# Transposing attention probabilities in one DMA per pair or in two, with another spread of the gate steps

## The chip, the cores and the metric

The kernel runs on one core of a Trainium2 chip. The core has five engines that run their own instruction streams: TensorE (PE; PEld is its weight load), VectorE (DVE), ScalarE (ACT), GpSimd (POOL) and SyncE (SP), which here only issues DMAs. The metric is the device time of one execution in microseconds; smaller is better.

## The reference

One decoder layer over 1024 positions of width 1024. Two groups of eight heads read the same input projection: multi-head latent attention (MLA, causal), and a dilated sliding-window attention in which three windows are mixed. Each group has a SiLU gate; then come one output projection, the residual and a layer norm.

```python
h = x @ w_in
c_q, c_kv, k_rope, g_a, q_b, k_b, v_b, g_b = split(h)
y_a = mla_attention(c_q, c_kv, k_rope, ...) * silu(g_a)      # p = softmax(q k), then p @ v
y_b = dilated_attention(q_b, k_b, v_b) * silu(g_b)           # three dilations, combined
x   = layernorm(ALPHA * x + concat(y_a, y_b) @ w_out)
```

## The kernel before

Products are made in split precision: a high and a low part of each operand, three matmuls (`PASSES`) for each product. The order of work has four stages: the input projections, the dilated attention, MLA, and the output projection with the layer norm.

**Dilated stage.** `steps` lists 32 units `(hp, s, u)`: head pair, half of the sequence, block of 128 queries. For a unit, `dil_scores` (L606, L610) makes the scores of both heads `e`, L614 adds the mask and takes the row minimum on DVE, L620 is the exponential on ACT, `dil_high` (L638 to L643) scales and writes the high fp16 part, `dil_low` (L653, L655) the low part, on POOL or DVE. Both parts of two units that follow each other lie in one tile `p16` (names `p` in the profile). After every second unit one DMA transpose on SP's queue (L658) turns it into `ptd`: 24 blocks of 128x128 where `s` is 0, 32 where `s` is 1. `dil_values` (L686) multiplies the four units of a half with the values into `Od`.

**Gates among the units.** The 16 gates are products of the input with gate weights (L522, 24 matmuls each). They are generators: `next(fill)` does one step, half a gate of 12 matmuls. A unit does one step, and eight of the units do two. When gate (3, 0) is done, the latents `c`, tables and `u` are loaded (L705, L708, L759). After the gates come `gen_kpe`, `gen_k` and `gen_q`, which make the first keys and queries of MLA (L716, L730, L765, L768). Gate weights `wg` come by DMAs on ACT's queue (L116), are split by ACT (L75) and POOL (L76); there are three weight buffers and two for the raw data.

**MLA stage.** 64 units `(hp, ch, e, qi)`: head pair, chunk of 256 queries, head, query block in the chunk. `scores` (L804, L810), `expo` (L815), `high` (L831, L833) and `low` (L840 on POOL, L842 on DVE) give the high and low part of `n = 2*ch + qi + 1` key blocks. The two query blocks `qi` of a row `(hp, ch, e)` lie in one tile `ph` (the tag `p16`, three buffers for both stages), and when both are there, one DMA transpose on SP's queue (L844) turns 2 * (2n - 1) blocks, n that of `qi` 1, into `pT`: 6, 14, 22 or 30 for `ch` 0 to 3. `values` (L854) multiplies `pT` of both heads with the values into `O`.

**Output.** `project` (L953) and L1082 make the output projection from the gated results `ys` and the weights `wo`.

**What sets the order.** The lines above are recorded in program order, and a scheduler with its own costs then places all instructions on their engines; an edit in one place can so move rows anywhere behind it. Each engine then runs its rows strictly in order. DMAs of SP and ACT take eight completion semaphores (DMAHW0 to DMAHW7) in turn; a DMA waits until the one that had its semaphore before it has landed.

Of the kernel before, what the change touches and what calls it, by code (L numbers as in the profile page):

```python
# [40 lines left out]
def tile_hybrid_layer(ctx, tc, xT, xres, w_c, w_c2, w_vr, w_k, w_q, w_g, w_u, w_o,  # L41
                      qg, kvg, ln_g, ln_b, tabs, msk_mla, msk_dil, cs_dil, cs_pe, out):
    nc = tc.nc
    sync = nc.sync
# [281 lines left out]
    def pow2_find(vmx, nm, bank_=bank):  # L326
        m1 = small.tile([P, 1], F32, name=nm + "m1", tag="vm")
        nc.vector.tensor_reduce(m1, vmx, AX.X, ALU.max)
        find_pow2(m1, 2.0 ** -40, nm, bank_)

    def pow2(j, nm, inv, bank_=bank):

        e = common_pow2(nm, bank_)
        r = small.tile([P, 1], F32, name=nm + "r", tag="vm4")
        nc.vector.reciprocal(r, e)
        nc.vector.tensor_scalar(scl[:, j, 0:1], r, 2.0 ** 14, None, ALU.mult)
        nc.vector.tensor_scalar(scl[:, j, 1:2], e, 2.0 ** -14 * inv, None, ALU.mult)
# [63 lines left out]
    def mla_scales():  # L401

        ee, d = fs[:, 4:5], fs[:, 5:6]
        nc.vector.tensor_mul(ee, es[:, 1:2], es[:, 3:4])
        nc.vector.tensor_scalar(scl[:, 0, 1:2], ee, 2.0 ** -5 / PSC, None, ALU.mult)
        nc.vector.tensor_scalar(fs[:, 6:7], scl[:, 4, 1:2], 2.0, None, ALU.mult)
        nc.vector.scalar_tensor_tensor(d, ee, 2.0 ** 10, fs[:, 6:7], ALU.mult, ALU.max)
        nc.vector.reciprocal(fs[:, 6:7], d)
        nc.vector.tensor_scalar(fs[:, 2:3], fs[:, 6:7], 2.0 ** 15, None, ALU.mult)
        nc.vector.tensor_scalar(fs[:, 3:4], fs[:, 2:3], ee, 2.0 ** -24, ALU.mult, ALU.mult)  # L410
        nc.vector.tensor_mul(fs[:, 6:7], es[:, 0:1], es[:, 2:3])
        nc.vector.tensor_scalar(fs[:, 7:8], fs[:, 6:7], d, -SC_MLA * 2.0 ** -19, ALU.mult, ALU.mult)

    def load_qk(hp):
        QQ[hp] = qqp.tile([P, 2, T], F16, name=f"qq{hp}", tag="qq")
        KK[hp] = b8.tile([P, 3, T], F16, name=f"kk{hp}", tag="kk")
        for s in range(2):
            sync.dma_start_transpose(QQ[hp][:, :, half(s)], q_d[half(s), hp * 2 * P:(hp + 1) * 2 * P])
            yield
            sync.dma_start_transpose(KK[hp][:, :, half(s)], k_d[half(s), hp * 3 * P:(hp + 1) * 3 * P])  # L420
            yield
# [130 lines left out]
    VA, VB, TD, ST, P16, PTD = ({} for _ in range(6))  # L552

    def load_v(hp):
        VA[hp] = four(f"vA{hp}", [P, NB, 2, P])
        sync.dma_start(VA[hp], v_d[1][:, :, hp].rearrange("n p l c -> p n l c"))
        VB[hp] = four(f"vB{hp}", [P, 2, 4, 2, P])
        for c in range(4):
            sync.dma_start(VB[hp][32 * c:32 * c + 32].rearrange("a j r l c -> a (j r) (l c)"),
                           v_d[1][2 * c:2 * c + 2].rearrange("j (r a) g l c -> a g (j r) (l c)", a=32)[:, hp])  # L560
# [30 lines left out]
    def dil_scores(u_):  # L591

        hp, s, u = u_
        i, ns = 4 * s + u, 3 + s
        stt = ST[u_] = small.tile([P, 2, 4], F32, name=f"st{hp}{i}", tag="st", bufs=4)
        TD[u_] = four(f"td{hp}{i}", [P, 2, 512], F32)
        S = [ps_s.tile([P, 512], F32, name=f"Sd{hp}{i}{e}", tag="S")[:, :ns * P] for e in range(2)]

        for cls in range(2):
            for w, e in JOBS:  # L600
                rows = ME[e] if w else slice(0, P)
                q, kk = QQ[hp][rows, e], KK[hp][rows, 2 if w else e]
                if not cls:
                    rhs = kk[:, (i - 1) * P:(i + 1) * P] if i else \
                        kk[:, 0:P].unsqueeze(1).broadcast_to([rows.stop - rows.start, 2, P])
                    nc.tensor.matmul(S[e][:, (ns - 2) * P:], q[:, i * P:i * P + P], rhs, start=(w == 0), stop=False)  # L606
                    continue
                for r in range(4):
                    rhs = kk.rearrange("p (i r a) -> p r i a", r=4, a=32)[:, r, 0:4 * s + 4]
                    nc.tensor.matmul(S[e][32 * r:32 * r + 32, :(ns - 2) * P],  # L610
                                     q[:, i * P + 32 * r:i * P + 32 * r + 32], rhs, start=False, stop=(w == 1))
        mk = mdil[:, u if i else 4, (4 - ns) * P:]
        for e in range(2):
            nc.vector.tensor_tensor_reduce(TD[u_][:, e, :ns * P], S[e], mk, dsc[:, 1:2], BIG,  # L614
                                           ALU.add, ALU.min, stt[:, e, 0:1])
# [7 lines left out]
    def dil_inv(u_):  # L623
        stt = ST[u_]
        nc.vector.tensor_scalar(stt[:, :, 2], stt[:, :, 1], 1.0 / PSC, None, ALU.mult)
        nc.vector.reciprocal(stt[:, :, 3], stt[:, :, 2])  # L626

    def dil_high(u_):
        hp, s, u = u_
        ns = 3 + s  # L630
        if u % 2 == 0:
            P16[hp, s] = hp_.tile([P, 2, 2, 2, ns * P], F16, name=f"p16{hp}{s}{u}", tag="p16")
        p16 = P16[hp, s][:, u % 2]
        for e in range(2):
            t, h, sc = TD[u_][:, e, :ns * P], p16[:, e, 0], ST[u_][:, e, 3:4]
            w = WHO[u][e]
            if w == "P":
                nc.gpsimd.tensor_scalar(t, t, sc, 1.0, ALU.mult, ALU.mult)  # L638
                sc = 1.0
            if w == "Q":  # L640
                nc.gpsimd.tensor_scalar(h, t, sc, 1.0, ALU.mult, ALU.mult)
            else:
                nc.scalar.activation(h, t, AF.Copy, scale=sc)  # L643

    def dil_low(u_):
        hp, s, u = u_
        ns, p16 = 3 + s, P16[hp, s][:, u % 2]
        if u == 0:
            PTD[hp, s] = tp.tile([P, 4, 4 * ns, P], F16, name=f"ptd{hp}{s}", tag=f"pT{s}")
        for e in range(2):  # L650
            t = TD[u_][:, e, :ns * P]
            if WHO[u][e] == "P":
                nc.gpsimd.tensor_sub(p16[:, e, 1], t, p16[:, e, 0])  # L653
            else:
                nc.vector.scalar_tensor_tensor(p16[:, e, 1], t, ST[u_][:, e, 3:4], p16[:, e, 0],  # L655
                                               ALU.mult, ALU.subtract)
        if u % 2:
            sync.dma_start_transpose(PTD[hp, s][:, u - 1:u + 1].rearrange("p u z c -> p (u z) c"),  # L658
                                     P16[hp, s].rearrange("p u e l w -> p (u e l w)"))

    def dil_values(hp, s):
        g = GT[4 + hp, s]
# [29 lines left out]
    Q, K, U, PT, SM, TT, V, P16, PB = ({} for _ in range(9))  # L692
# [142 lines left out]
    def low(u):  # L835
        hp, ch, e, qi = u
        n, p16 = 2 * ch + qi + 1, P16[u]
        t = TT[u][:, :n * P].rearrange("p (n c) -> p n c", n=n)
        if n in POOLN:
            nc.gpsimd.tensor_sub(p16[:, :, 1], t, p16[:, :, 0])  # L840
        else:
            nc.vector.scalar_tensor_tensor(p16[:, :, 1], t, SM[u][:, 3:4], p16[:, :, 0], ALU.mult, ALU.subtract)  # L842
        if qi:
            sync.dma_start_transpose(PT[hp, ch][:, e], PB[hp, ch, e].rearrange("p n l c -> p (n l c)"))  # L844

    def values(hp, ch):
        O = gbank(f"O{hp}{ch}")[:, :256]
# [23 lines left out]
    for n in range(ND + 5):  # L871
        cur = steps[n] if n < ND else None
        old = steps[n - 1] if 1 <= n <= ND else None
        if n == 2:
            pow2_find(krm, "kr", gbank)
        if n == 5:
            pow2(4, "kr", 2.0 ** 14, gbank)
            mla_scales()
            nc.vector.tensor_scalar(scl[:, 0, 2:3], scl[:, 0, 1:2], 0.5, None, ALU.mult)
        if cur:  # L880
            if cur[1:] == (0, 1) and 0 < cur[0] < PAIRS - 1:
                qks = load_qk(cur[0] + 1)
            next(qks, None)
            if cur[1:] == (1, 0) and cur[0]:
                load_v(cur[0])
            dil_scores(cur)
        if old:
            dil_inv(old)
            dil_high(old)
            dil_low(old)  # L890
        if cur:
            for e in range(2):
                dil_expo(cur, e)
            for _ in range(1 + (n % 3 == 0 and n < 24)):
                next(fill, None)
        if n == ND + 3:
            for _ in fill:
                pass
        m = n - DV
        if 0 <= m < ND and m % 4 == 3:  # L900
            dil_values(*steps[m][:2])
# [60 lines left out]
    for n in range(NU + 8):  # L962
        if n < NU:
            hp, ch, e, qi = units[n]
            z = n % 16
# [103 lines left out]
    for i in ROWS:  # L1069
# [5 lines left out]
        for c in range(2):  # L1075
            if i in HALVED:
                n = 1 + (i == ROWS[-1])
                for z in ((0, 512),) if n == 1 or c == 0 else ((0, 256), (256, 512)):
                    p = gbank(f"op{i}{c}{z[0]}")
# [119 lines left out]
```

## Time and profile before

| | us |
|---|---|
| median of 3 runs | 653.58 (650.23 to 655.44) |
| profiled execution | 648.14 |
| its span, first to last instruction | 646.3 |
| PE busy | 594.8 (92% of the span) |
| DVE busy | 398.2 (62%) |
| ACT busy | 320.0 (50%) |
| POOL busy | 299.1 (46%) |

Busy is time in which an engine has an instruction under way. A busy PE is not a PE at its peak, since matmuls are pipelined and their ends are modelled. Chain rows tell what the end of the program followed from, step by step; a wait row tells which engine's idle time a given producer ended.

### The profile page before, as it was taken

What the parts mean: (1) busy time and instruction counts of PE and PEld (TensorE: products, weight loads), DVE (VectorE), ACT (ScalarE), POOL (GpSimd) and SP (SyncE); (2) the same over time, 40 slices, a digit from 0 to 9 for tenths busy, and PEclk for the clock granted to TensorE, in tenths of its full rate; (3) what the DMA queues carried; (4) which work ended last, traced back from release to release, by engine and by line L of the source; (5) the groups of instructions that cost most, each with busy time, mean ns of one, the idle gap of its engine ahead of it and who ended that gap; (6) DMA issues with size and microseconds to landing.
All of it is one profiled execution on the core that took longest, in us unless ns stands there. A gap on an engine that the chain in (4) does not pass through costs nothing. (4 is left out here: it accounts for less than half of the span.)

```text
span 646.3 us, 11099 instructions
## 1 busy us (share of the span) xinstructions
PE 594.8 (92%) x4046; PEld 435.7 (67%) x4046; DVE 398.2 (62%) x890; ACT 320.0 (50%) x645; POOL 299.1 (46%) x326
## 2 busy tenths in 40 slices
PE   8999998999999899999997987887989977999995
PEld 5888886788999366776764644434545546778884
DVE  3425318480541686644644897678898997365696
ACT  4452136554221386545636575577978787340000
POOL 3374754265331227534644757373758566450000
PEclk9999999999999999999997997988999987999999
DMA  6666137796012779993999996549798899752042
GB/s 198 188 198 198 30 97 204 221 289 174 33 66 74 260 233 144 184 208 78 225 296 234 184 212 147 108 94 185 150 159 163 173 199 225 185 154 81 17 163 98
DMA packets 198663, 105.52 MB, mean 163 GB/s; under 512 B 157520, under 2 KB 175568, under 8 KB 198480
## 3 DMA queue, kind: packets, MB, share of 16 engines
q1 hardware_dynamic: 195008, 99.11, 64.7%
q10 hardware_dynamic: 3600, 5.71, 3.4%
q8 instruction: 31, 0.51, 0.3%
q14 instruction: 24, 0.20, 0.1%
HBM read 47.65 MB, written 18.35 MB: 102 GB/s over the span
## 5 line engine op out<-in xcount | busy, mean ns | idle before, releaser
L522 PE MATMUL gP<-x,wg 128*128 128x512 f32 x384 | 98.8, 406 | 5.9 <-ACT wg L75 5.5
L522 PEld LDWEIGHTS gP<-x,wg 128*128 128x128 f32 x384 | 70.7, 191 | 23.2 <-ACT wg L75 6.1
L953 PE MATMUL op<-wo,ys 128*128 128x512 f32 x288 | 70.7, 401 | 0.6 <-ACT ys L75 0.4
L953 PEld LDWEIGHTS op<-wo,ys 128*128 128x128 f32 x288 | 54.3, 191 | 14.4 <-ACT ys L75 0.9
L815 ACT ACTIVATE p<-p,sm 128x128 f32<-128x128 f32 (+3 forms) x64 | 49.1, 767 | 22.1 <-DVE sm L810 17.3
L804 PE MATMUL S<-k,q 128*128 128x512 f16 (+3 forms) x288 | 54.7, 339 | 5.2 <-DVE sm L810 4.8
L253 PE MATMUL cP<-x,wc 128*128 128x512 f32 x240 | 56.7, 395 | 0.0
L810 DVE CUSTOM_DVE_ANT_0 p<-S,mask,fs 128x128 f32<-128x128 f32 (+3 forms) x64 | 50.5, 809 | 4.7 <-POOL ph L840 3.4
L253 PEld LDWEIGHTS cP<-x,wc 128*128 128x128 f32 x240 | 44.7, 188 | 10.3
L620 ACT ACTIVATE td<-td,st 128x384 f32<-128x384 f32 (+1 forms) x64 | 42.1, 659 | 16.6 <-DVE st L614 16.4
L638 POOL TENSOR_SCALAR td<-td,st 128x384 f32<-128x384 f32 (+1 forms) x32 | 22.5, 710 | 56.9 <-DVE st L626 44.4
L804 PEld LDWEIGHTS <-q 128*128 128x128 f16 x288 | 26.7, 101 | 30.8 <-issue 5.7
L614 DVE CUSTOM_DVE_ANT_0 td<-Sd,mdil,dsc 128x384 f32<-128x384 f32 (+1 forms) x64 | 41.3, 679 | 9.1 <-PE Sd L610 8.9
L168 PE MATMUL acc<-wq,x 128*128 128x512 f32 x192 | 45.1, 395 | 0.9 <-DVE x L155 0.8
L854 PE MATMUL O<-pT,v 128*64 128x256 f16 (+1 forms) x480 | 33.1, 285 | 13.9 <-DMA pT<-ph 11.4
L129 PE MATMUL qkP<-wk,x 128*128 128x512 f32 x192 | 44.5, 393 | 0.0
L840 POOL TENSOR_TENSOR ph<-p,ph 128x256 f16<-128x256 f32 (+3 forms) x32 | 36.6, 1153 | 15.6 <-ACT ph L833 12.4
L854 PEld LDWEIGHTS <-v 128*64 128x64 f16 x480 | 28.8, 119 | 22.1 <-issue 18.4
L842 DVE SCALAR_TENSOR_TENSOR ph<-p,sm,ph 128x128 f16<-128x128 f32 (+3 forms) x32 | 35.0, 1101 | 13.8 <-ACT ph L833 13.8
L168 PEld LDWEIGHTS acc<-wq,x 128*128 128x128 f32 x192 | 36.0, 188 | 10.5 <-DVE x L155 1.3
L129 PEld LDWEIGHTS qkP<-wk,x 128*128 128x128 f32 x192 | 36.0, 188 | 8.2
L653 POOL TENSOR_TENSOR p<-td,p 128x384 f16<-128x384 f32 (+1 forms) x32 | 35.7, 1124 | 11.4 <-ACT p L643 11.2
(313 smaller groups left out, 1158.7 us busy)
## 6 DMA issues: line engine op xcount, KB each, us to landing
u<-in_w_u_dram SPq DMA_DIRECT2D x20, 256.0 KB, 3.1
v_d<-v SPq DMA_DIRECT2D x16, 256.0 KB, 2.1
wor<-in_w_o_dram SPq DMA_DIRECT2D x8, 512.0 KB, 4.2
xr<-in_xres_dram SPq DMA_DIRECT2D x16, 256.0 KB, 3.1
out_dram<-xr SPq DMA_DIRECT2D x16, 256.0 KB, 2.1
xr<-in_xT_dram SPq DMA_DIRECT2D x15, 256.0 KB, 3.0
k_d<-k SPq DMA_DIRECT2D x8, 384.0 KB, 4.4
c_d<-c SPq DMA_DIRECT2D x10, 256.0 KB, 2.4
```

The costliest lines, as they stand in the source:

```text
L129: nc.tensor.matmul(d, xs[k][i // 4][:, a, (i % 4) * P:(i % 4) * P + P], w8[k][:, b, o:o + w], **flags(k, KD, (a, b)))
L168: nc.tensor.matmul(acc[i], xs[k][i // 4][:, a, (i % 4) * P:(i % 4) * P + P], ws[:, b, :512], start=(k == 0 and (a, b) == (0, 0)), stop=(k ...
L253: nc.tensor.matmul(dst, ww(k, a, m), xs[k][s][:, b], **flags(k, KD, (a, b)))
L522: nc.tensor.matmul(p, wg[k // 4][:, a, (k % 4) * P:(k % 4) * P + P], xs[k][s][:, b], **flags(k, KD, (a, b)))
L614: nc.vector.tensor_tensor_reduce(TD[u_][:, e, :ns * P], S[e], mk, dsc[:, 1:2], BIG, ALU.add, ALU.min, stt[:, e, 0:1])
L620: nc.scalar.activation(t[:, :w], t[:, :w], AF.Exp, bias=ST[u_][:, e, 0:1], scale=-1.0, accum_out=ST[u_][:, e, 1:2])
L804: nc.tensor.matmul(S[:, lo:hi], q[:, a, qc], k[:, b, lo:hi], start=((a, b) == (0, 0)), stop=((a, b) == (1, 0)))
L810: nc.vector.tensor_tensor_reduce(t[:, :w], S[:, :w], M["mask"][:, T - w:], fs[:, 7:8], BIG, ALU.add, ALU.min, sm[:, 0:1])
L815: nc.scalar.activation(TT[u][:, :w], TT[u][:, :w], AF.Exp, bias=SM[u][:, 0:1], scale=-1.0, accum_out=SM[u][:, 1:2])
L840: nc.gpsimd.tensor_sub(p16[:, :, 1], t, p16[:, :, 0])
L854: nc.tensor.matmul(O[ME[e], q0:], V[hp][:, kb, vh, ME[e]], rhs, **flags(kb, 2 * ch + 2, (vh, phl)))
L953: nc.tensor.matmul(op[i][:, half(c)], ys[k][a][:, i * P:(i + 1) * P], ws[k][b][:, half(c)], **flags(n_, KD, (a, b)))
```

## The change

Each transpose becomes two. In the dilated stage each unit is turned by itself (12 or 16 blocks), right after its `dil_low`; in MLA each query block of a row (2n blocks: 2 and 4, 6 and 8, 10 and 12, 14 and 16). Tiles and buffers stay as they are. The number of transposes of probabilities goes from 16 + 32 to 32 + 64, the blocks stay the same. The eight units with two gate steps were units 0, 3, 6, ... 21 and are now 0, 2, 4, ... 14. By either rule the 32 gate steps end with unit 23.

```diff
@@ dil_low
-        if u % 2:
-            sync.dma_start_transpose(PTD[hp, s][:, u - 1:u + 1].rearrange("p u z c -> p (u z) c"),
-                                     P16[hp, s].rearrange("p u e l w -> p (u e l w)"))
+        sync.dma_start_transpose(PTD[hp, s][:, u], p16.rearrange("p e l w -> p (e l w)"))
@@ low
-        if qi:
-            sync.dma_start_transpose(PT[hp, ch][:, e], PB[hp, ch, e].rearrange("p n l c -> p (n l c)"))
+        z = 2 * qi * (n - 1)
+        sync.dma_start_transpose(PT[hp, ch][:, e, z:z + 2 * n], p16.rearrange("p n l c -> p (n l c)"))
@@ main loop of the dilated stage
-            for _ in range(1 + (n % 3 == 0 and n < 24)):
+            for _ in range(1 + (n % 2 == 0 and n < 16)):
                 next(fill, None)
```

Lines behind L658 have a number smaller by 1 or 2 in the changed kernel (L844 is L842, L658 is L657, L708 is L706).

The first place is SP's queue in MLA, at chunks 1 to 3 of the first head pair. A row is one DMA; `pT` is the target, `ph` the tile with the probabilities of one row, and the middle number the blocks. Before:

```order
L844 DMA_TRANSPOSE pT_4755<-ph_4858 128x14x128
L844 DMA_TRANSPOSE pT_4820<-ph_4904 128x22x128
L844 DMA_TRANSPOSE pT_4820<-ph_4964 128x22x128
L844 DMA_TRANSPOSE pT_4922<-ph_4994 128x30x128
L759 DMA u_5610<-u_d_75 128x2048
L844 DMA_TRANSPOSE pT_4922<-ph_5059 128x30x128
```

After the change:

```order
L842 DMA_TRANSPOSE pT_4839<-ph_4924 128x10x128
L842 DMA_TRANSPOSE pT_4772<-ph_4877 128x6x128
L842 DMA_TRANSPOSE pT_4772<-ph_4877 128x8x128
L842 DMA_TRANSPOSE pT_4839<-ph_4924 128x12x128
L842 DMA_TRANSPOSE pT_4839<-ph_4985 128x10x128
L757 DMA u_5202<-u_d_74 128x2048
L842 DMA_TRANSPOSE pT_4839<-ph_4985 128x12x128
L842 DMA_TRANSPOSE pT_4943<-ph_5016 128x14x128
L842 DMA_TRANSPOSE pT_4943<-ph_5016 128x16x128
L842 DMA_TRANSPOSE pT_4943<-ph_5082 128x14x128
L842 DMA_TRANSPOSE pT_4943<-ph_5082 128x16x128
```

Each row has become two, and the 10 blocks of chunk 2 now go ahead of the second head of chunk 1.

The second place is the loading of the latents on SP's queue and of the last gate weights on ACT's, late in the dilated stage, with the semaphores that a row waits for. Before, SP:

```order
L708 DMA c_3660<-c_d_67 128x2048 [waits DMAHW3_49,PE_49]
L708 DMA c_3661<-c_d_68 128x2048 [waits DMAHW4_49,PE_49]
L708 DMA c_3662<-c_d_69 128x2048 [waits DMAHW5_49,PE_49]
L708 DMA c_3663<-c_d_70 128x2048 [waits DMAHW6_49,PE_49]
L708 DMA c_3664<-c_d_71 128x2048 [waits DMAHW7_49,PE_49]
L705 DMA tab<-in_tabs_dram 128x512 [waits DMAHW0_49,PE_49]
L759 DMA u_3667<-u_d_72 128x2048 [waits DMAHW1_49,PE_49]
L705 DMA tab<-in_tabs_dram 128x512 [waits DMAHW2_49]
L556 DMA vA_3694<-v_d_66 128x8x256 [waits DMAHW3_49]
```

Before, ACT, whose next gate weights are `wg20r` and `wg21r`:

```order
L116 DMA wg20r<-in_w_g_dram 128x512 [waits DMAHW5_49,Activation_49]
L643 ACTIVATE p_3651<-td_3624,st_3623 128x384 [waits DVE_49,Activation_49]
L620 ACTIVATE td_3702,st_3701<-td_3702,st_3701 128x512 [waits DVE_49,Pool_49]
L620 ACTIVATE td_3702,st_3701<-td_3702,st_3701 128x512 [waits DVE_49]
L116 DMA wg21r<-in_w_g_dram 128x512 [waits DMAHW3_49]
L532 ACTIVATE g_3753<-gP_3675 128x512 [waits PE_49]
```

After the change, SP:

```order
L706 DMA c_3631<-c_d_67 128x2048 [waits DMAHW0_49,PE_49]
L706 DMA c_3632<-c_d_68 128x2048 [waits DMAHW1_49,PE_49]
L706 DMA c_3633<-c_d_69 128x2048 [waits DMAHW2_49,PE_49]
L657 DMA_TRANSPOSE ptd_3573<-p_3569 128x12x128 [waits DMAHW3_49,DVE_49,DMAHW5_49,PE_49,Pool_49]
L757 DMA u_3638<-u_d_72 128x2048 [waits DMAHW4_49,PE_49]
L706 DMA c_3634<-c_d_70 128x2048 [waits DMAHW5_49]
L706 DMA c_3635<-c_d_71 128x2048 [waits DMAHW6_49]
L657 DMA_TRANSPOSE ptd_3573<-p_3569 128x12x128 [waits DMAHW7_49,DVE_49,Pool_49]
L703 DMA tab<-in_tabs_dram 128x512 [waits DMAHW2_49]
```

After the change, ACT:

```order
L116 DMA wg20r<-in_w_g_dram 128x512 [waits DMAHW0_49]
L643 ACTIVATE p_3693<-td_3596 128x384 [waits DMAHW6_49,Pool_49]
L643 ACTIVATE p_3693<-td_3596 128x384 [waits Pool_49]
L620 ACTIVATE td_3666,st_3665<-td_3666,st_3665 128x384 [waits DVE_49] x2
L116 DMA wg21r<-in_w_g_dram 128x512 [waits DMAHW1_49]
L532 ACTIVATE g_3720<-gP_3646 128x512 [waits PE_49]
```

The semaphore of `wg21r` was last taken by the load of `vA`, behind eight other loads; now by the second of the `c` loads.

The third place is DVE between the last dilated units and the first of MLA: L614 is a score row of the dilated stage, `k` and `qf` are the first keys and queries of MLA. Before (the last score row stands two rows ahead of these):

```order
L625 TENSOR_SCALAR st_4425<-st_4425 128x2
L735 SCALAR_TENSOR_TENSOR k_4062<-kg_4178,fs,k_4062 64x512
L625 TENSOR_SCALAR st_4462<-st_4462 128x2
L914 MEMSET mask 128x1024
L735 SCALAR_TENSOR_TENSOR k_4062<-kg_4225,fs,k_4062 64x512
L626 RECIPROCAL st_4425<-st_4425 128x2
L626 RECIPROCAL st_4462<-st_4462 128x2
L687 SCALAR_TENSOR_TENSOR g_2941<-Od_4542,scl,g_2941 128x512
L625 TENSOR_SCALAR st_4498<-st_4498 128x2
L915 COPY mask<-mmla 128x128
L655 SCALAR_TENSOR_TENSOR p_4453<-td_4296,st_4295,p_4453 128x512
L768 SCALAR_TENSOR_TENSOR qf_4283<-qg_4273,tab 128x512
```

After the change:

```order
L733 SCALAR_TENSOR_TENSOR k_4073<-kg_4238,fs,k_4073 64x512
L614 ISA td_4440,st_4439<-Sd_4441,mdil,dsc 128x512
L614 ISA st_4439 128x1
L625 TENSOR_SCALAR st_4309<-st_4309 128x2
L766 SCALAR_TENSOR_TENSOR qf_4297<-qg_4287,tab 128x512
L614 ISA td_4440,st_4439<-Sd_4442,mdil,dsc 128x512
L614 ISA st_4439 128x1
L614 ISA td_4478,st_4477<-Sd_4479,mdil,dsc 128x512
```

The first `qf` stood behind the last score row of the dilated stage and now stands ahead of the last three units' rows.

## Rows read from the trace of the kernel before

**Rows 1.** Windows by stage: length; busy us of PE, PEld, DVE, ACT, POOL; PEclk; DMA.

```profile
232.00:345.00 113.00, 110.14 (x986) 76.60 (x984) 63.51 (x178) 64.14 (x147) 57.45 (x60) 1.00 0.94 197
345.00:403.00 58.00, 48.36 (x460) 29.37 (x461) 47.29 (x101) 37.79 (x85) 37.54 (x42) 0.88 0.94 184
403.00:458.00 55.00, 44.40 (x357) 24.95 (x357) 39.77 (x99) 39.38 (x86) 28.00 (x32) 0.94 0.70 134
458.00:541.00 83.00, 70.35 (x554) 42.10 (x550) 76.49 (x156) 66.87 (x126) 55.10 (x47) 0.96 0.91 169
541.00:646.30 105.30, 97.02 (x493) 77.73 (x491) 66.81 (x132) 20.10 (x39) 20.55 (x14) 0.97 0.42 129
```

**Rows 2.** Waits of PE over the span: us in total, times, longest.

```profile
PE O L854 <- DMA pT<-ph: 11.4, 6, 2.7
PE gP L522 <- ACT wg L75: 5.5, 2, 4.5
...
PE Od L686 <- DMA ptd<-p: 2.3, 1, 2.3
```

**Rows 3.** Waits for transposes between 403 and 458 us.

```profile
PE O L854 <- DMA pT<-ph: 3.3, 2, 1.9
...
ACT ph L833 <- DMA pT<-ph: 1.9, 1, 1.9
```

**Rows 4.** Waits for transposes between 458 and 541 us.

```profile
PE O L854 <- DMA pT<-ph: 8.1, 4, 2.7
...
ACT ph L833 <- DMA pT<-ph: 2.4, 3, 1.0
```

**Rows 5.** Chain that ended last: start, length, what (DMAs from issue to landing).

```profile
437.52 6.81 DMA pT<-ph
...
476.98 8.24 DMA pT<-ph
...
528.64 11.77 DMA pT<-ph x2
```

**Rows 6.** L844 on SP in four windows: 6 blocks; two of 22; 30; 30.

```profile
L844 SPq DMA_TRANSPOSE pT<-ph x1: 1209/1209/1209, 486.9 to 486.9; - x1
...
DMA to landing us min/median/max: 2.8/2.8/2.8
...
L844 SPq DMA_TRANSPOSE pT<-ph x2: 3370/3377/3384, 468.4 to 471.9; - x2
...
DMA to landing us min/median/max: 5.2/5.3/5.3
...
L844 SPq DMA_TRANSPOSE pT<-ph x1: 5147/5147/5147, 537.4 to 537.4; - x1
...
DMA to landing us min/median/max: 6.5/6.5/6.5
...
L844 SPq DMA_TRANSPOSE pT<-ph x1: 4509/4509/4509, 477.0 to 477.0; - x1
...
DMA to landing us min/median/max: 8.2/8.2/8.2
```

**Rows 7.** Timeline late in the dilated stage: start, length, instruction [idle before <-releaser].

```profile
337.09 0.62 ACT L643 ACTIVATE p<-td,st 128x384 f16<-128x384 f32 x1 [3.49 <-DMA c<-c_d]
...
345.38 0.33 ACTq L116 DMA_DIRECT2D wg21r<-in_w_g_dram  x1
345.76 0.60 ACT L532 ACTIVATE g<-gP 128x512 f32<-128x512 f32 x1 [5.12 <-DMA vA<-v_d]
...
348.04 0.80 PE L522 MATMUL gP<-x,wg 128*128 128x512 f32 x1 [4.54 <-ACT wg L75]
```

**Rows 8.** The window around that wait, columns as in rows 1.

```profile
346.60:353.40 6.80, 5.36 (x19) 3.37 (x20) 5.65 (x18) 5.68 (x15) 3.76 (x4) 0.50 1.16 179
```

**Rows 9.** Timeline of PE: one gate step early in the dilated stage.

```profile
279.71 3.04 PE L522 MATMUL gP<-x,wg 128*128 128x512 f32 x12
```

**Rows 10.** Waits of SP's queue over the span.

```profile
SPq L844 <- POOL ph L840: 25.8, 10, 9.4
```

## The prediction

> **What bounds the kernel now.** I read the stages first [rows 1]. From 232 to 345 us PE is busy in 110.1 of 113.0 us: it is the bound, and what makes data ready sooner there gives nothing. From 345 on PE is idle for 9.6 us (58.00 - 48.36), then 10.6, 12.7 and, in the output stage, 8.3. The work of PE is not changed by this edit, so the time can fall only by these idle times and by stretches at the lower clock (PEclk is 0.88 to 0.96 between 345 and 541). The second column to see is DVE: from 458 to 541 it is busy in 76.5 of 83.0 us. If PE gets its data sooner there, DVE soon holds it again, since its work stays; only 6.5 us can be had. From 403 to 458 DVE is free for 15.2 us and is no such lid.
>
> Then I asked for what PE waits. Transposed probabilities are its largest wait: 11.4 us in six waits in MLA, and 2.3 us in one in the dilated stage [rows 2]. 3.3 us of the six lie ahead of 458, 8.1 behind it, and ACT waits for the same transposes (it needs their source buffer back) 1.9 and 2.4 us [rows 3, 4]. The chain of waits agrees: single transposes stand in it with 6.81, 8.24 and, two together, 11.77 us [rows 5]. The second largest wait of PE is for gate weights, 5.5 us in two [rows 2], of which one is 4.54 us at 348 [rows 7].
>
> **The change part by part.**
>
> *A transpose by size.* With nothing behind them, 6 blocks land 2.8 us after their issue, 22 blocks 5.2, 30 blocks 6.5; they hold SP's queue for 1.21, 3.38 and 5.15 us [rows 6]. (5.2 - 2.8) / 16 and (6.5 - 2.8) / 24 both give some 0.15 us a block, on 1.9 us that each one has. By this the last piece of a row lands sooner than the whole would: 16 blocks for 30 gain 14 x 0.15 = 2.1 us, 12 for 22 gain 1.5, 8 for 14 gain 0.9; in the dilated stage 12 for 24 gain 1.8. The first piece can go while the second query block is still being worked on.
>
> *What the 48 new transposes cost.* The floor on SP's queue is 1.21 us, seen with 6 blocks; pieces of 2 and 4 will not be cheaper. In MLA the 24 rows of chunks 1 to 3 only divide time that the queue spends anyway. The eight rows of chunk 0 take 2 x 1.21 for 1.21: 9.7 us of SP's time, spread over 140 us. What hides it: SP's queue stands waiting for the low parts, 25.8 us for POOL's alone [rows 10]. If that cover were gone, the 9.7 us would delay whatever is queued behind, which are the loads of `u`, `v` and `wo`. I take 0 and keep up to +3 for the range. The Trainium skill speaks against splitting: in "DMA: Bandwidth & Descriptors", Rules for kernel authors, it says to coalesce many small transfers, because under 64 KB one pays mostly overhead, and a piece of two blocks is just 64 KB. By that rule the 48 pieces would cost their 1.9 us each, 91 us of DMA time. The trace bears out the 1.9 us but not that they add up: 22 blocks issued at 471.9 us, 3.5 us behind other 22 that took 5.2 to 5.3 to land, landed as fast as those [rows 6].
>
> *Term 1, MLA ahead of 458 us.* Two waits of PE, 1.9 and 1.4 us in the 3.3 [rows 3], behind 22 and 30 blocks: 1.5 and 1.4 of them can go. ACT's 1.9 us, behind 14 blocks, loses 0.9. That is 3.8 at most; ACT's and PE's waits lie on one chain through the same rows, and what comes next is DVE, which must finish its rows for the following chunk. I take -2.5, with 0 and -3.8 as ends.
>
> *Term 2, MLA from 458 to 541 us.* Of the 8.1 us [rows 4], the longest wait (2.7) is behind 22 blocks and loses 1.5; the other three, 5.4 together, are behind 30, and lose up to 2.1 each, some 5: 6.5 in all. The lid is DVE's 6.5 us of idle time [rows 1], not all of which can be used, as it has its own waits for ACT. I take -3.0, ends 0 and -6.5.
>
> *Term 3, the dilated stage.* The one wait of 2.3 us [rows 2] is behind 24 blocks; 1.8 could go. I take -1.5, ends 0 and -1.8. The other transposes of this stage have no one waiting.
>
> *Term 4, the gate weights at 348 us.* This goes by the rearrangement, not by the split. ACT's queue stood for 3.49 us until a load of `c` had landed, then issued `wg20r`, then stood again for 5.12 us until `vA` had landed, because the DMA of `wg21r` takes over its semaphore. So `wg20r` lay in its buffer while ACT could not split it, and PE waited 4.54 us [rows 7]. Behind that PE ran for 6.8 us at PEclk 0.50, which is 1.2 GHz, with 5.36 us busy [rows 8]: some 2.7 us lost. In the new order both loads take over semaphores of the first two `c` loads, which are ahead of all the others, so the second stop should go. PE also comes to that gate a little sooner after gate (3, 0), which works the other way. Bounds: -7.2 (4.5 + 2.7) if it all goes, 0 if the weights are as late as before. I take -3.5.
>
> *Term 5, the gates' double steps.* A step holds PE for 3.04 us [rows 9]. By the new rule 24 steps instead of 22 fall in the first sixteen units, so two steps, 6.1 us of PE's work, move from units 16 to 23, where PE has room to be idle, into a stretch where PE is full. Nothing is lost while PE is full, but the weights must come faster: the waits for weights ahead of 345 are 5.5 - 4.5 = 1.0 us now, and I expect that to double, +1. And 6.1 us fewer are there to fill PE's idle time behind 345. The first keys and queries of MLA move up into the same stretch, and should fill most of it; I take +1, with -2 and +6 as ends.
>
> Sum: -2.5 - 3.0 - 1.5 - 3.5 + 2.0 = -8.5 us. The profiled execution took 648.14 us, so it would be 639.6. It stands 5.4 us below the median of the runs, 653.58; the same step from there gives **645.1 us**, 1.3% less.
>
> **The rivals.**
>
> *The wait moves to DVE, and the rearrangement gives nothing.* Then PE's waits for transposes turn into waits for score banks, which DVE empties. For it speaks the 92% of DVE from 458 to 541 [rows 1], against it the 15.2 us that DVE is free before. The gain is term 1 alone: 653.6 - 2.5 = 651.
>
> *The gates' new places cost more than they give.* PE would stand for weights ahead of 345, or behind it with nothing to fill: the +6 of term 5 against terms 1 to 3 (-7.0) and no term 4: 652 to 653. For it speaks that PE has caught up with its weights twice already [rows 2]; against it, that 1.0 us in 113 is little.
>
> *Slower: transposes that follow each other hold each other up.* The place is SP's queue in MLA. The 30 blocks issued at 477.0 landed after 8.2 us, not 6.5, with other 30 blocks behind them at once [rows 6]: 1.7 us more. When every row is two pieces, nearly each has one right behind it. If this 1.7 us comes with each piece, it eats the 0.9 to 2.1 us by which the last piece is shorter, and the first piece of the next row is late too, so ACT gets its buffers later than now. Ten waits (six of PE, four of ACT [rows 3, 4]) longer by 0.6 to 1.2 us give +6 to +12: 660 to 666, with 660 as the value. It decides from the point at which a piece of 16 takes over 6.5 us to land. Against it speak the two rows of 22, which did not hold each other up. The Trainium skill has a rule to this end ("Perfetto Trace Analysis", DMA Optimizations): splitting may let a task end sooner if DMA engines are generally idle. Here their share is 0.91 from 458 to 541 [rows 1], so by that rule the gain is in doubt.
>
> **How the numbers follow.** A measurement of this kernel can hardly tell 1% from no change, 6.5 us (647.0 to 660.1 counts as the same). The forecast has 0.53, with 637 to 649 as its own range; 0.46 of it lies below 647. The rival with DVE has 0.22 (0.02 below 647, the rest the same), the one with the gates 0.12 (0.02 of it slower), the slow one 0.13 (0.12 slower, 0.01 the same). Faster 0.48, the same 0.38, slower 0.14. If every term came to its good end, -3.8 - 6.5 - 1.8 - 7.2 - 2 = -21 or 632; I cut the range at 635. Above, it reaches to 658, past the two rivals that stay within 1% and the +3 of the queue; the slow rival is left out for the most part.
>
> **What would show it right or wrong.** PE's waits for `pT` should fall from 11.4 us to 3 to 6, that for `ptd` to under 1, and pieces of 16 blocks should land in 4.2 to 5 us. Around the second load of `wg20r` and `wg21r`, ACT should stand once, not twice, and PE's wait there be under 2 us, with no 6.8 us at half clock behind it. DVE's busy share in MLA should rise. PE should stay over 95% busy up to 345 us; a fall there is the gates' rival. The output stage should be as long as now. Wrong it would be through a new wait that the scheduler's order makes in a place that I have not weighed: every engine's order differs from the dilated stage on.

## The result, and the profile after

The change made the kernel slower: 670.1 us (median of 4 runs, 667.0 to 673.0) against 653.1 (650.2 to 655.4), ratio 1.027, 95% interval 1.022 to 1.031. That is 17 us, where 8.5 less were forecast. The profiled executions lie further apart (672.32 and 648.14), so sums over their stages show some 24 us.

To see where the time goes, both spans are cut where PE had done the same work (its busy time weighted with the granted clock: 240, 300, 340, 380 and 500 us of it). Windows of the kernel before; the columns are as in [rows 1]: length, busy us of PE and of the others, PEclk, DMA share.

```profile
248.00:309.00 61.00, 59.65 (x512) 42.24 (x512) 33.08 (x94) 33.92 (x75) 32.05 (x33) 1.00 0.82 153
309.00:356.00 47.00, 42.46 (x408) 28.30 (x406) 24.07 (x62) 25.39 (x60) 22.49 (x25) 0.93 1.13 247
356.00:406.00 50.00, 42.74 (x428) 25.94 (x421) 41.37 (x85) 30.64 (x70) 33.24 (x38) 0.93 0.92 184
406.00:557.00 151.00, 128.01 (x990) 78.11 (x988) 122.21 (x264) 111.40 (x219) 88.08 (x81) 0.94 0.83 164
557.00:646.30 89.30, 81.41 (x398) 65.46 (x396) 59.40 (x119) 13.20 (x25) 13.49 (x7) 0.98 0.33 107
```

The same work in the changed kernel:

```profile
249.00:320.00 71.00, 64.01 (x491) 45.08 (x490) 31.53 (x85) 33.92 (x75) 33.77 (x34) 0.93 0.78 139
320.00:361.00 41.00, 40.45 (x392) 27.07 (x391) 21.37 (x58) 23.37 (x53) 21.15 (x22) 1.00 0.98 227
361.00:413.00 52.00, 45.10 (x453) 25.47 (x452) 38.04 (x86) 32.77 (x75) 29.28 (x34) 0.87 0.90 185
413.00:578.00 165.00, 133.80 (x1001) 76.43 (x996) 133.74 (x281) 115.14 (x228) 94.39 (x91) 0.90 0.82 159
578.00:670.50 92.50, 84.74 (x414) 68.75 (x412) 58.48 (x120) 13.84 (x26) 14.07 (x8) 0.97 0.36 111
```

Two numbers of each row matter: PE's idle time (length less busy) and what the lower clock costs at most ((1 - PEclk) x length).

| PE's work from/to | before: idle + clock | after: idle + clock |
|---|---|---|
| 240 to 300, first dilated units | 1.3 + 0 | 7.0 + 5.0 |
| 300 to 340 | 4.5 + 3.3 | 0.5 + 0 |
| 340 to 380, last dilated units | 7.3 + 3.5 | 6.9 + 6.8 |
| 380 to 500, MLA | 23.0 + 9.1 | 31.2 + 16.5 |
| 500 to the end | 7.9 + 1.8 | 7.8 + 2.8 |

The second row is the gain that term 4 forecast, and larger. It is lost again in the first row (10.7 us more), where PE was full before, and in MLA (15.6 us more). By the sums of the two columns 9.4 us more are idle (53.4 against 44.0), and up to 13.4 us more (31.1 against 17.7) go to TensorE's lower clock.

PE's waits in the changed kernel (us in total, times, longest; they answer to [rows 2]):

```profile
PE S L802 <- DVE sm L808: 11.6, 12, 4.1
PE Od L684 <- DMA ptd<-p: 10.6, 4, 5.4
PE O L852 <- DMA pT<-ph: 10.0, 4, 5.2
...
PE gP L522 <- ACT wg L75: 3.1, 3, 2.1
```

The waits that the split was to shorten did not shrink: `pT` 10.0 for 11.4, `ptd` 10.6 for 2.3. The first line was, in the kernel before:

```profile
PE S L804 <- DVE sm L810: 4.8, 4, 3.1
```

The first place of the loss is visible in PE's timeline after the change (start, length, instruction, and in brackets the idle time before it):

```profile
259.11 0.64 PE L610 MATMUL Sd<-kk,qq 128*32 128x256 f16 x16
263.56 0.61 PE L684 MATMUL Od<-ptd,vB 128*64 128x128 f16 x7 [3.81 <-DMA ptd<-p]
...
267.53 12.26 PE L522 MATMUL gP<-x,wg 128*128 128x512 f32 x48
```

Seven value matmuls `Od` stand right behind the scores of unit 6, and the scores of unit 7, then 48 gate matmuls and the scores of unit 8 queue behind them. What followed, with columns as above, is half clock (1.2 GHz) with PE nearly always busy:

```profile
263.10:269.90 6.80, 6.34 (x41) 3.65 (x42) 3.06 (x16) 2.50 (x6) 1.40 (x3) 0.50 0.55 112
```

In the kernel before, PE reaches the same `Od` among the scores of unit 8, one and a half units later in its order, and its bulk only behind the 48 gate matmuls; it waits for nothing:

```profile
258.15 0.24 PE L686 MATMUL Od<-ptd,vB 128*64 128x128 f16 x1
...
259.08 0.24 PE L686 MATMUL Od<-ptd,vB 128*64 128x128 f16 x1
259.26 11.17 PE L522 MATMUL gP<-x,wg 128*128 128x512 f32 x48
270.36 0.81 PE L686 MATMUL Od<-ptd,vB 128*64 128x128 f16 x22
```

PE took none of the ready work behind `Od`. The Trainium skill states this ("PSUM — Partial Sum Buffer", Engine vs sequencer instructions): a weight load may overlap matmuls that are in flight, but matmuls start and complete in program order. The trace agrees, with its 3.81 us.

The data is late there too. ACT's order has the split of a gate weight (L75) ahead of the high parts of units 2 and 3, and its load takes 7.6 us (issued 243.0):

```profile
250.68 0.62 ACT L75 CAST wg<-wg51r 128x512 fp32r<-128x512 f32 x1 [5.18 <-DMA wg51r<-in_w_g_dram]
```

Before, the same instruction waited for nothing:

```profile
244.86 0.60 ACT L75 CAST wg<-wg51r 128x512 fp32r<-128x512 f32 x1
```

So the last piece of the first half landed at 263.3 us, against 257.4 for the last pair before, although that stretch began only 3 us later (PE's scores there start at 240.1 and 237.1).

### The profile page after: what moved, and what is told of

The parts are those of the page before. It is cut to its first block, busy times and chain, and to the rows that moved or that the text cites. A ratio compares the mean times of both kernels' runs of the same rounds, so it can differ in the third digit from the quotient of the medians.

```text
span 670.5 us, 11237 instructions
## 1 busy us (share of the span) xinstructions
PE 610.2 (91%) x4046; PEld 439.2 (66%) x4046; DVE 398.9 (59%) x890; ACT 320.4 (48%) x645; POOL 296.4 (44%) x326
## 5 line engine op out<-in xcount | busy, mean ns | idle before, releaser
L522 PE MATMUL gP<-x,wg 128*128 128x512 f32 x384 | 101.5, 415 | 3.7 <-ACT wg L75 3.1
L522 PEld LDWEIGHTS gP<-x,wg 128*128 128x128 f32 x384 | 72.9, 197 | 22.0 <-ACT wg L75 3.6
L802 PE MATMUL S<-k,q 128*128 128x512 f16 (+3 forms) x288 | 57.4, 345 | 11.7 <-DVE sm L808 11.6
L614 DVE CUSTOM_DVE_ANT_0 td<-Sd,mdil,dsc 128x384 f32<-128x384 f32 (+1 forms) x64 | 41.5, 679 | 24.5 <-PE Sd L610 20.0
L168 PE MATMUL acc<-wq,x 128*128 128x512 f32 x192 | 47.1, 408 | 0.8 <-DVE x L155 0.8
L168 PEld LDWEIGHTS acc<-wq,x 128*128 128x128 f32 x192 | 37.6, 196 | 10.8 <-DVE x L155 1.3
L852 PEld LDWEIGHTS <-v 128*64 128x64 f16 x480 | 26.4, 115 | 22.1 <-issue 15.1
L840 DVE SCALAR_TENSOR_TENSOR ph<-p,sm,ph 128x128 f16<-128x128 f32 (+3 forms) x32 | 37.2, 1173 | 5.2 <-ACT ph L831 5.0
```

Of the source, the lines that this page charges most:

```text
L168: nc.tensor.matmul(acc[i], xs[k][i // 4][:, a, (i % 4) * P:(i % 4) * P + P], ws[:, b, :512], start=(k == 0 and (a, b) == (0, 0)), stop=(k ...
L522: nc.tensor.matmul(p, wg[k // 4][:, a, (k % 4) * P:(k % 4) * P + P], xs[k][s][:, b], **flags(k, KD, (a, b)))
L802: nc.tensor.matmul(S[:, lo:hi], q[:, a, qc], k[:, b, lo:hi], start=((a, b) == (0, 0)), stop=((a, b) == (1, 0)))
L852: nc.tensor.matmul(O[ME[e], q0:], V[hp][:, kb, vh, ME[e]], rhs, **flags(kb, 2 * ch + 2, (vh, phl)))
```

## The experiments

The change has three parts: D (split in the dilated stage), M (split in MLA), G (the gates' new places). Ratios are to runs of the kernel before made beside each, with 95% intervals; 0.1% is 0.65 us. The change and dil_gates have 4 runs each, the others 10.

| | parts | median us | ratio |
|---|---|---|---|
| the change | D M G | 670.1 | 1.0268 (1.0222 to 1.0314) |
| split_only | D M | 657.4 | 1.0090 (1.0057 to 1.0124) |
| gates_only | G | 654.1 | 1.0031 (0.9988 to 1.0074) |
| split_dil | D | 654.6 | 1.0048 (1.0009 to 1.0086) |
| split_mla | M | 653.2 | 0.9999 (0.9959 to 1.0040) |
| dil_gates | D G | 665.2 | 1.0204 (1.0119 to 1.0288) |
| mla_gates | M G | 649.3 | 0.9947 (0.9904 to 0.9990) |
| hold_od | D M G, `Od` held | 658.9 | 1.0088 (1.0050 to 1.0126) |
| hold_all | D M G, `Od` and `O` held | 655.3 | 1.0036 (0.9994 to 1.0078) |
| split_hold_od | D M, `Od` held | 654.9 | 1.0048 (1.0012 to 1.0085) |
| split_hold_all | D M, `Od` and `O` held | 651.1 | 0.9987 (0.9948 to 1.0026) |
| mg_hold_o | M G, `O` held | 650.7 | 0.9992 (0.9963 to 1.0022) |
| before_hold_o | `O` held | 648.8 | 0.9972 (0.9931 to 1.0012) |

**The parts, one or two at a time.** *split_only*, against the changed kernel (G undone):

```diff
-            for _ in range(1 + (n % 2 == 0 and n < 16)):
+            for _ in range(1 + (n % 3 == 0 and n < 24)):
```

> Both transposes are split, the gates' double steps stay at units 0, 3, 6 to 21. Three theories. G, the gates' new places are the loss (they put gate work ahead of the low parts of the first dilated units, whose transposes come 17 to 20 us later): 642 to 653 us here, the split itself being worth 0 to -10. S, the split is the loss (more transposes on SP's queue, each with its wait): 665 to 672, as with the whole change. O, neither alone, only the order that the scheduler makes of both together: 648 to 656, and the same for the three other kernels of this group.

*gates_only*, against the kernel before:

```diff
-            for _ in range(1 + (n % 3 == 0 and n < 24)):
+            for _ in range(1 + (n % 2 == 0 and n < 16)):
```

> Transposes stay one per pair and row, only the gates' double steps go to units 0, 2, 4 to 14. G: 665 to 675, with the transposes of the first dilated units late by some 20 us. S: 650 to 656, no difference. O: 650 to 656.

*split_dil*, against the kernel before:

```diff
-        if u % 2:
-            sync.dma_start_transpose(PTD[hp, s][:, u - 1:u + 1] ...
+        sync.dma_start_transpose(PTD[hp, s][:, u], p16.rearrange("p e l w -> p (e l w)"))
```

> Only the transposes of the dilated stage are split, gates as before. G: 648 to 655. S: some of the 17 us, since the marks of the two traces part in the dilated stage: 660 to 670 if the loss is there. O: 650 to 656.

*split_mla*, against the kernel before:

```diff
-        if qi:
-            sync.dma_start_transpose(PT[hp, ch][:, e], PB[hp, ch, e] ...
+        z = 2 * qi * (n - 1)
+        sync.dma_start_transpose(PT[hp, ch][:, e, z:z + 2 * n], p16.rearrange("p n l c -> p (n l c)"))
```

> Only the transposes of MLA are split, gates as before. G: 645 to 653. S: 655 to 660 if the pieces of MLA hold each other up on SP's queue (PE's waits for pT would stay at 10 to 11 us), 650 to 654 if the loss is in the dilated stage. O: 648 to 656.

No part alone costs more than 0.5%. G as the whole loss (665 to 675 alone) and S, the split as the whole loss (665 to 672 for D and M), both fell. The third came nearest, but D and M together already cost 0.9%, which it did not allow.

*dil_gates*, against the changed kernel, is M undone:

```diff
-        z = 2 * qi * (n - 1)
-        sync.dma_start_transpose(PT[hp, ch][:, e, z:z + 2 * n], ...
+        if qi:
+            sync.dma_start_transpose(PT[hp, ch][:, e], ...
```

> The split of the dilated stage with the gates' new places; MLA's transposes stay one per row. In the changed kernel PE's rows have the first value matmuls (Od) two units earlier than before, and again one unit earlier at 371 us; the transposes land sooner than before there, but PE, which runs strictly in order, stands for them. Theory P (these two places, made by the order of these two parts together, and a worse order at the end of MLA, made by all three): the dilated part of the loss is here, 659 to 666. Rival C (MLA's pieces on SP's queue are needed for the loss): 650 to 656.

*mla_gates*, against the changed kernel, is D undone:

```diff
-        sync.dma_start_transpose(PTD[hp, s][:, u], ...
+        if u % 2:
+            sync.dma_start_transpose(PTD[hp, s][:, u - 1:u + 1] ...
```

> The split of MLA with the gates' new places; the dilated stage's transposes stay one per pair. P: no early Od without the split of the dilated stage, so 651 to 657. C: a good part of the loss, 658 to 666.

D and G together cost 2.0%, four times D's 0.5% and more than the sum with G's 0.3%; without D the other two cost nothing (mla_gates is even 0.5% faster, its interval just clear of 1). So most of the loss needs the dilated split and the gates' places together, and MLA's pieces (rival C) are not needed. PE's timelines agree. dil_gates has the same `Od` ahead of unit 7, and waits:

```profile
260.56 0.61 PE L684 MATMUL Od<-ptd,vB 128*64 128x128 f16 x7 [2.24 <-DMA ptd<-p]
```

In gates_only the first `Od` stands ahead of unit 8, one unit later, and waits for nothing:

```profile
258.43 0.36 PE L686 MATMUL Od<-ptd,vB 128*64 128x128 f16 x6
```

mla_gates has the same order as gates_only there, and both have PE busy in all of the 68 us from 250 to 318. One sentence of the expectation was wrong: the transposes do not land sooner at that place, as shown above.

**The same kernel with another order on PE.** *hold_od* is the changed kernel with PE's order pinned: `Od` may not be issued ahead of the last score matmul that precedes it in the program (order only, no wait for data added).

```diff
-                    nc.tensor.matmul(S[e][32 * r:32 * r + 32, :(ns - 2) * P],
+                    LS["d"] = nc.tensor.matmul(S[e][32 * r:32 * r + 32, :(ns - 2) * P],
...
-            dil_values(*steps[m][:2])
+            with tc.issue_after(LS["d"].ins):
+                dil_values(*steps[m][:2])
```

> The changed kernel with one thing more: in PE's order the value matmuls of the dilated stage stay behind the scores that precede them in the program, as they are in the kernel before. Work, transposes and waits for data stay the same; PE's order differs in the two places where Od was early. P: PE's waits for ptd fall from 10.6 to 2 to 4 us and the half clock behind them goes, so 8 to 13 us less than the changed kernel, 657 to 663. C: the wait only changes its name (scores or gate weights come late), 667 to 673.

The time fell by 1.8%, 11.7 us. At the first place PE now does scores and gate matmuls while the same transposes are under way (timeline, columns as above):

```profile
259.41 0.51 PE L611 MATMUL Sd<-kk,qq 128*32 128x256 f16 x8
259.85 11.17 PE L522 MATMUL gP<-x,wg 128*128 128x512 f32 x48
270.87 0.61 PE L607 MATMUL Sd<-kk,qq 128*128 128x256 f16 x4
```

The windows of the same work (the first, third and fourth stretch):

```profile
250.00:310.00 60.00, 59.65 (x487) 42.24 (x487) 31.49 (x87) 32.17 (x72) 32.18 (x34) 1.00 0.86 156
...
351.00:403.00 52.00, 45.94 (x463) 25.26 (x462) 40.97 (x90) 33.07 (x73) 32.28 (x38) 0.87 1.02 190
403.00:564.00 161.00, 129.33 (x989) 76.01 (x988) 126.79 (x273) 113.22 (x225) 91.18 (x87) 0.94 0.83 160
```

The first stretch is 11 us shorter and has lost its idle time and its half clock, from the place of 15 matmuls. That is most of the 15.7 us by which the two profiled executions differ (spans of 670.5 and 654.8); 4 us more come from MLA, where the clock is 0.94 instead of 0.90. The second early `Od` was not cured: in the third stretch PE still stands 6.1 us, and waits for `ptd` total 7.7 us, not 2 to 4.

*hold_all* pins `O` of MLA in the same way.

```diff
-                nc.tensor.matmul(S[:, lo:hi], q[:, a, qc], k[:, b, lo:hi],
+                LS["s"] = nc.tensor.matmul(S[:, lo:hi], q[:, a, qc], k[:, b, lo:hi],
...
-            values(*units[n - VL][:2])
+            with tc.issue_after(LS["s"].ins):
+                values(*units[n - VL][:2])
```

> The same for the value matmuls of MLA too (O behind the scores that precede them in the program). P: another 2 to 8 us less than with Od alone, since the waits of 4.1 and 5.2 us at the end of MLA stand at readers that were put ahead of ready scores: 652 to 659. If the waits of MLA are set by DVE and by the transposes themselves, no difference to the kernel with Od alone.

It gave 0.5% more (3.4 us), about the width of its interval. What it is aimed at stands at the end of MLA in the changed kernel:

```profile
544.50 3.68 PE L802 MATMUL S<-k,q 128*128 128x512 f16 x9 [4.09 <-DVE sm L808]
...
562.71 0.39 PE L852 MATMUL O<-pT,v 128*64 128x256 f16 x1 [5.24 <-DMA pT<-ph]
563.03 1.14 PE L802 MATMUL S<-k,q 128*128 128x128 f16 x6
```

A single `O` waits 5.24 us, with the last scores behind it. In the pinned kernel no wait of PE in MLA is longer than 4.7 us; its idle time there is the same (157.0 - 125.7 = 31.3 us, row below), the clock 0.95 instead of 0.90 (0.94 with `Od` alone pinned). The profiled execution of hold_all took 659.3 us, 4 above its median, so its stages can't be compared to the microsecond, and how the pin of `O` works is not shown by them.

**The pins without G, and without D.** *split_hold_od* and *split_hold_all* have the two diffs above on split_only, *mg_hold_o* the second on mla_gates, *before_hold_o* the second on the kernel before.

> Both splits, gates as before, and Od held behind the scores that precede it in the program. Theory P (early Od is the cost of the dilated part): with both splits alone PE lost 8.3 us to idling and half clock from 250 to 318 us against 1.3 in the kernel before; that goes here, so 650 to 654 instead of 657. If Od's place matters only together with the gates' new places: no change, 656 to 659.

> The same, with O of MLA held behind the scores that precede it too. P: another 2 to 4 us less, as with the changed kernel: 647 to 651. If the gain from holding O was only a chance of that one order: within 2 us of the kernel that holds Od alone.

> MLA's split with the gates' new places (the fastest so far), and O held. P, if an early O costs in any order: 645 to 648. If O's waits there are set by DVE and the transposes themselves: 648 to 651.

> The kernel before with O of MLA held and nothing else changed: 12 waits of PE in MLA stand at an O whose transposes are not there yet. If holding O helps by itself, 647 to 650 and all that the hold gave in the changed kernel is unrelated to the split; if the kernel before has its O where it should be, 651 to 655.

Pinning `Od` gives 0.4% without G (1.0090 to 1.0048, about an interval) and 1.8% with it. With G the order put `Od` ahead of unit 7, without G ahead of unit 8. That fits, but does not explain all of it: in the profiled executions the pin saves 11.6 us of idle time and clock in the first stretch with G (12.0 to 0.4) and 6.4 without (split_only 8.6, split_hold_od 2.2), and why only 2.5 us of the 6.4 reach the median is not shown. Nor is the place alone the cost: gates_only has `Od` ahead of unit 8 too, with its data there. A reader that is early and data that is late, by the split, are both needed. With both pins and without G the split kernel is as fast as the kernel before. Pinning `O` gave another 0.6% there, as in hold_all, but nothing on mla_gates (0.9947 to 0.9992, the wrong way) and 0.3%, inside the interval, on the kernel before. So a pinned `O` helps in the orders that both splits make, twice by about the same, and is no rule for any order.

What G costs with both pins is the step from split_hold_all to hold_all, 0.5%. It lies among the last dilated units. Windows of hold_all, the third and fourth stretch:

```profile
353.00:407.00 54.00, 46.34 (x461) 26.20 (x462) 40.11 (x92) 33.37 (x75) 30.86 (x35) 0.84 0.97 196
407.00:564.00 157.00, 125.71 (x990) 74.27 (x987) 130.69 (x275) 113.70 (x225) 94.24 (x89) 0.95 0.85 160
```

The same of split_hold_all:

```profile
353.00:396.00 43.00, 39.83 (x454) 23.20 (x447) 36.79 (x81) 30.31 (x70) 29.82 (x35) 1.00 0.94 193
396.00:555.00 159.00, 127.95 (x998) 75.22 (x997) 132.54 (x279) 115.59 (x230) 95.48 (x88) 0.95 0.84 164
```

The third stretch is 43 us instead of 54. These two executions lie 10.7 us apart (spans of 657.5 and 646.8) and the medians 4.2, so the size of the cost is taken from the ratios and only its place from here. In hold_all PE stands there for a dilated transpose (first line), and so it does in hold_od (second line), whose profiled execution was faster than its median and has 52 us for this stretch, as shown above:

```profile
367.34 0.85 PE L685 MATMUL Od<-ptd,vB 128*64 128x128 f16 x12 [6.40 <-DMA ptd<-p]
...
361.24 0.85 PE L685 MATMUL Od<-ptd,vB 128*64 128x128 f16 x12 [4.90 <-DMA ptd<-p]
```

From the scores of unit 23 to this `Od`, PE's order holds 2 gate matmuls with G and 14 without it: two of the gate steps that covered the transposes have been used up before unit 16. With the pins and without G no wait for `ptd` is left among PE's waits.

Together: 1.0268, less 0.0180 for the place of `Od`, 0.0052 for that of `O`, 0.0049 for the gates' places, is 0.9987. In this order of undoing them, the three add up to the loss; the last two steps are each about as large as an interval, but their sum (1.0088 to 0.9987) is clear.

## Why the prediction was wrong, step by step

**The step that failed** is the one by which the dilated stage ahead of 345 us could neither gain nor lose: PE was full there, so its new order was costed only for gate weights (term 5, at most +6), and term 3 took it that nobody waits for the stage's other transposes. PE was full because its order kept most of `Od` behind 48 gate matmuls, and the change took that away: `Od` went ahead of unit 7, where it had been among unit 8, while its data came 6 us later. The prediction's last sentence names such a wait as what would make it wrong, but gave it no place and no price; it weighed the new orders of SP, ACT and DVE, and not that of PE. Pinning `Od` back is worth 11.7 us (hold_od) of the 25.5 between forecast and result.

**Terms 1 and 2 (MLA, -5.5)** came to nothing: M alone is 0.9999. The pieces are as quick as worked out. In split_mla, a row of 14 and 16 blocks issued at 481.2 and 484.1:

```profile
L844 SPq DMA_TRANSPOSE pT<-ph x2: 1785/2298/2812, 481.2 to 484.1; - x2
...
DMA to landing us min/median/max: 4.1/4.2/4.3
```

But in this part of MLA the first piece has little head start. The low parts of both query blocks of a row end 1.6 us apart already in the kernel before (DVE, 475.3 and 476.9 us):

```profile
474.17 1.15 DVE L842 SCALAR_TENSOR_TENSOR ph<-p,sm,ph 128x896 f16<-128x896 f32 x1 [0.22 <-ACT ph L833]
...
475.63 1.28 DVE L842 SCALAR_TENSOR_TENSOR ph<-p,sm,ph 128x1024 f16<-128x1024 f32 x1
```

So the second piece queues behind the first, and in split_mla the row before took 6.1 and 6.5 us to land, issued at 475.4 and 477.3. Counted from the end of the last low part, the rows of 30 blocks are there sooner by 0.8 and 2.4 us (485.2 - 476.9 = 8.3 and 489.1 - 481.0 = 8.1 before; 483.8 - 476.3 = 7.5 and 488.4 - 482.7 = 5.7 with M), where the terms had 2.1. PE does not get it: its readers come sooner too (the `O` behind the second of these rows waits 1.25 us at 488.5, where it waited 0.83 at 489.1), its waits for `pT` total 14.0 us (11.4 before), and those for score banks, which DVE empties, rise from 4.8 to 7.0. That bears out the first rival, which had 0.22, in part: the waits for score banks grew, but those for `pT` did not turn into them, and term 1, which it kept, did not come either.

**Term 3 (-1.5)** holds only where `Od` is pinned and the gates stay: no wait for `ptd` is left in split_hold_od and split_hold_all. In the changed kernel it became +8.3 of waiting.

**Term 4 (-3.5)** was right in mechanism and low in size. PE's wait for gate weights there is

```profile
354.06 0.73 PE L522 MATMUL gP<-x,wg 128*128 128x512 f32 x2 [0.55 <-ACT wg L75]
```

with no half clock behind it, and ACT no longer stands for `c` or `vA`. The stretch lost 0.5 us instead of 7.8, as much as the bound of -7.2. It is the split of the dilated stage that gives this order: the stretch loses 7.7 us in gates_only, where ACT still stands 5.6 us for `c`, and 2.4 in split_dil, where it stands for neither.

**Term 5 (+2)** was right in size for what it weighed: with `Od` pinned G costs 0.4 and 0.5% (hold_od against split_hold_od, hold_all against split_hold_all), 2.6 and 3.2 us, each no larger than its interval, and by the mechanism of the second rival, gate steps that are missing as cover behind 345. Without the pins it costs 1.6 to 1.8%, by the place of `Od`.

**The 48 transposes** cost nothing that a time shows, as taken: 32 of them are in M alone (0.9999), all 48 in split_hold_all (0.9987). The rule of the Trainium skill that was cited ("DMA: Bandwidth & Descriptors", Rules for kernel authors) says to coalesce many small transfers, since under 64 KB one pays mostly overhead. That the overheads add up, 91 us, was the prediction's reading of it; no run here bears that out, and the smallest piece is 64 KB, so none lies below the rule's figure.

**The slow rival** named a time near the one measured (660 to 666) by a mechanism that is not there: the longest of the 64 pieces took 6.2 us to land in the changed kernel, under the 6.5 from which it was to decide, and M alone loses nothing.

**The signs to look for**: `pT` 10.0 (3 to 6 expected) and `ptd` 10.6 (under 1) were wrong; PE's share up to 345 fell to 106.0 of 113.0 us, 94%, which was to be the sign of the gates' rival and is that of the early `Od`; DVE's share in MLA, which was to rise, stayed at 81% (122.2 of 151, 133.7 of 165 us); PE idles in the last stretch as long as before, as expected (7.8 and 7.9 us), though the stretch is 3.2 us longer.

**Open**: that the gate weight's place in ACT's order makes the first transposes late is read from the timeline, and no run undoes it alone. hold_od has the same order there (ACT stands 3.40 us for `wg51r`), and with `Od` pinned its first stretch loses only 0.4 us, so late data costs nothing there as long as no reader stands for it. In MLA, cut by PE's work as above, PE idles 27 to 34 us in the eight kernels with D and 23 to 28 in the six without (31.1 in split_hold_all, 159.0 - 127.9, against 23.0 before), which takes back most of what the split gains ahead of MLA (by idle time and clock, split_hold_all loses 11.4 us less than the kernel before ahead of MLA and 6.9 more in it). Why that order of MLA is worse was not found beyond the `O` that was pinned.

## What to carry to other kernels

Where a scheduler sets the order, a change that makes data ready in pieces also moves the readers, and on an engine that runs in order a reader that is a few rows early costs its wait, the ready work behind it and TensorE's clock. So compare the order of the full engine first, reader by reader against the work that used to cover its data, and try a pin of the reader behind that work when it has moved; measure each pin, since here that of `Od` paid 1.8 and 0.4%, and that of `O` 0.5 and 0.6% in two orders and nothing clear in two others. A transfer that is quicker by 1 or 2 us gives little if its two parts become ready nearly together and the next wait, here for DVE, is right behind it.

## What the runs showed of the hardware

In the changed kernel a granted clock of 0.50 (1.2 GHz) began in a wait of 3.81 us and held from 263.1 to 269.9 us, with PE busy again in 6.34 of these 6.80 us; in its first stretch the lower clock cost up to 5.0 us beside 7.0 us of idle time. A load of one gate weight, issued at 243.0 us beside two transposes and five other loads, took 7.6 us to land; the next one, issued at 250.75 when the loads had landed and the transposes nearly so, took 2.6 us.
